# One hybrid decoder layer in fp32 on one core: asking for the weight residues of three projection groups one or two chunks earlier

## The chip, the core and the metric

The kernel runs on one core of one Trainium2 chip. The metric is the device time of one execution in microseconds. A core has a matmul engine (PE), a vector engine (DVE), a scalar engine (ACT), a general engine (POOL) and a queue that issues the loads (SP). Each works through its own list of instructions in order, and they wait for each other through semaphores.

## What is computed

The reference is one decoder layer for 256 tokens of width 1024, in fp32. Two causal token mixers share one RMS-normed input and one combined projection: A, eight heads that share one key and value head and attend to the 64 keys per token that a small indexer picks; B, eight heads with keys and values of their own (with 256 tokens there is one block, so B is plain causal attention). Their outputs are concatenated and go through one output projection; then come a SwiGLU feed-forward block, a gated embedding and a last norm. Cut to what matters here:

```
a = rmsnorm(h, g_attn)
proj = a @ w_in                      # 2500 columns: qa ka va qi ki wi qb kb vb
y_a = dsa_attention(qa, ka, va, qi, ki, wi)   # relu indexer, top 64 keys, softmax
y_b = moba_attention(qb, kb, vb)              # causal softmax
h = h + concat(y_a, y_b) @ w_out
h = h + (silu(f @ w_gate) * (f @ w_up)) @ w_down      # f = rmsnorm(h)
h = h + sigmoid(u @ w_ple_gate) * (p @ w_ple_proj)    # u = rmsnorm(h)
out = rmsnorm(h, g_final)
```

## The kernel before

Every fp32 matrix product is done in three passes of a reduced format: a matrix is split into `hi`, its cast to that format, and `lo`, the residue `raw - hi`; the product is hi x hi + hi x lo + lo x hi. So each weight chunk takes three steps ahead of the matmuls. SP loads `raw` from memory (line 120, at most 1 MB), ACT casts it to `hi` (line 131), DVE subtracts and leaves `lo` (line 158). A chunk of 2048 columns is cast and subtracted in two halves of 1024, which are the rows `128x1024` of the views; the first half serves the first two row blocks k of the chunk, the second half the other two. Chunks have a fixed list (`CHUNKS`), and `raw`, `hi` and `lo` have three buffers each, used in turn.

Chunks 5 and 6 are projection group 2 (kb), 7 and 8 group 3 (vb), 9 and 10 group 4 (qa), 11 is the weight `pp` of the embedding and 12 to 15 are `wo`, the output projection. So `lo8` is the residue of group 3's second chunk, `hi12` the cast of the first `wo` chunk, and so on.

`need(kind, k0)` is called where the matmuls of a chunk are written. It calls `load(i + LOOK)`, which records the loads and casts up to three chunks ahead, and `split(i)`, which records the residues up to chunk i and no further. PE's order is that of the code, since only PE is scheduled by hand; on DVE and ACT a scheduler places instructions by the order in which the code records them and by its own estimate of when each can run. So the place where `split` is called decides where DVE's residue work stands among the other work of DVE.

Around the change the code runs group 1 (qb), evacuates group 0, runs group 2 (kb), turns its result (`evac_rope`, lines 325 to 332, the rope of kb), runs group 3 (vb) and then group 4 (qa). Within a group, PE does six matmuls of 512 columns for each of eight steps (two row blocks, three passes, one half t of the tokens). Between the steps of groups 3 and 4 stand parts of the attention, hung in by a table (`at_tick`): transposes of `qb`, of the indexer's heads (`tidx`) and of `kb`, the indexer's products (`qki`, then `rel` on ACT and `score` on DVE), the logits of B's three units (`qk_b`, then `lg`, `pr` and the transposes `pt_b`). The top-k of the indexer's scores (lines 427 and 428: MAX of eight keys and their replacement, eight rounds for each half of the tokens) makes the mask `dmask` for A's units, which follow while the output projection runs (`qk_a`, `lg_a`, `pr_a`, `pt_a`).

Of the kernel before, what the change touches and what calls it, by code (L numbers as in the profile page):

```python
# [62 lines left out]
def layer_kernel(  # L63
# [39 lines left out]
    def load(upto):  # L103
        while state["hi"] <= min(upto, len(chunks) - 1):
            i = state["hi"]
            kind, k0, src, nk, cw = chunks[i]
            n = nk * cw
            if nk == 1:
                raw = a2.tile([P, n], F32, tag="pr", name=f"raw{i}", bufs=4)
            elif kind == "g1":  # L110

                if k0 < 6:
                    if k0 == 2:
                        state["g1"] = act.tile([P, 2048], F32, tag="yH", name="raw_g1")
                    raw = state["g1"][:, (k0 - 2) // 2 * n : (k0 // 2) * n]
                else:
                    raw = act.tile([P, n], F32, tag="yL", name=f"raw{i}")
            else:
                raw = wp.tile([P, 2048], F32, tag="raw", name=f"raw{i}")
            nc.sync.dma_start(raw[:, :n], src)  # L120
            if i == len(chunks) - 1:
                hi = state["ff"].tile([P, 2048], F32R, tag="hidH", name=f"hi{i}", bufs=1)
            elif nk == 1:
                hi = a2.tile([P, n], F32R, tag="rt2", name=f"hi{i}")
            elif kind == "g1":
                hi = at.tile([P, n], F32R, tag={2: "qbT", 4: "kbT", 6: "vb"}[k0], name=f"hi{i}")
            else:
                hi = wp.tile([P, 2048], F32R, tag="hi", name=f"hi{i}")
            step = cw * max(1, min(nk, 1024 // cw))
            for o in range(0, n, step):  # L130
                nc.scalar.copy(hi[:, o : o + step], raw[:, o : o + step])  # L131
            tiles[i] = (raw, hi)
            state["hi"] += 1

    def split(upto):
        load(upto)
        while state["lo"] <= min(upto, len(chunks) - 1):
            i = state["lo"]
            kind, k0, src, nk, cw = chunks[i]
            n = nk * cw  # L140
            raw, hi = tiles.pop(i)
            if i == len(chunks) - 1:
                lo = state["ff"].tile([P, 2048], F32R, tag="hidL", name=f"lo{i}", bufs=1)
            elif nk == 1:
                lo = a2.tile([P, n], F32R, tag="r0", name=f"lo{i}")
            elif kind == "g1":
                if k0 < 6:
                    if k0 == 2:
                        state["g1l"] = act.tile([P, 2048], F32R, tag="pp", name="lo_g1")
                    lo = state["g1l"][:, (k0 - 2) // 2 * n : (k0 // 2) * n]  # L150
                else:
                    lo = at.tile([P, n], F32R, tag="idxT", name=f"lo{i}")
            else:
                lo = wp.tile([P, 2048], F32R, tag="lo", name=f"lo{i}")
            step = cw * max(1, min(nk, 1024 // cw))
            for o in range(0, n, step):
                e = o + step
                nc.vector.tensor_tensor(  # L158
                    lo[:, o:e], raw[:, o:e], hi[:, o:e].bitcast(F32), op=ALU.subtract
                )  # L160
            ready[i] = (
                hi[:, :n].rearrange("p (k w) -> p k w", k=nk),
                lo[:, :n].rearrange("p (k w) -> p k w", k=nk),
            )
            state["lo"] += 1

    def need(kind, k0):
        i = index[(kind, k0)]
        load(i + LOOK)
        split(i)  # L170
        return ready[i]

    def mm3(ps, aH, aL, wH, wL, start, stop):
# [96 lines left out]
    with actx:  # L270
# [29 lines left out]
        def piece(g, pss, k, ts):  # L300

            if g == 0:
                (wH, wL), r = g0[k], slice(None)
            else:
                c0 = max(c[1] for c in chunks if c[0] == f"g{g}" and c[1] <= k)
                wH, wL = need(f"g{g}", c0)
                wH, wL = wH[:, k - c0, :], wL[:, k - c0, :]
            width = wH.shape[1]
            for n, (aT, wT) in enumerate(((XH, wH), (XL, wH), (XH, wL)) if len(ts) > 1 and k else ((XH, wH), (XH, wL), (XL, wH))):
                for t in ts:  # L310
                    nc.tensor.matmul(  # L311
                        pss[t][:, :width], aT[:, k, tsl(t)], wT,
                        start=k == 0 and n == 0, stop=k == KD - 1 and n == 2,
                    )
# [274 lines left out]
        for t in range(NT):  # L589
            for c in range(2):  # L590
                ps = acc(f"pp{t}{c}")
                wH, wL = need("pp", 0)
                cc = slice(c * NQ, (c + 1) * NQ)
                for k in range(2):
                    mm3(ps, pTH[:, k, tsl(t)], pTL[:, k, tsl(t)], wH[:, k, cc], wL[:, k, cc], k == 0, k == 1)
                nc.scalar.copy(pp[:, t, cc], ps)
                tick("pp", 2 * t + c)
# [4 lines left out]
        def wo_mms(kk, t, c):  # L602
            wH, wL = need("wo", kk - kk % 2)
            cc = slice(c * NQ, (c + 1) * NQ)
            mm3(po[(t, c)], yH[:, kk, tsl(t)], yL[:, kk, tsl(t)], wH[:, kk % 2, cc], wL[:, kk % 2, cc], kk == 4, kk == 3)
# [6 lines left out]
        i = 0  # L612
# [276 lines left out]
```

## Time and profile before

| what | value |
|---|---|
| median of 3 runs | 341.28 us (340.81 to 341.32) |
| the profiled execution | 342.88 us |
| its span, first to last instruction | 341.0 us |
| mean granted clock of PE | 0.984 |
| PE busy | 327.8 us (96%) |
| DVE busy | 227.7 us (67%) |
| ACT busy | 174.3 us (51%) |

The span is what the views show; the execution's own time has 1.88 us more around it. The granted clock is 1 where PE runs at 2.4 GHz and 0.5 where it runs at 1.2. In the timeline a row has the start in us from the span's start, the duration, the engine, the line, the operation, out<-in, the shapes, the number of instructions in the row, and in brackets the idle time ahead of it with what ended it. Matmuls overlap, so the distance of two starts, and not the duration, is what one costs.

### The profile page before, as it was taken

To read this page: it belongs to the slowest core of one execution; us is meant where nothing else is said; L and a number is where in the kernel's file an instruction comes from. 1 tells how busy PE (TensorE), PEld (TensorE's weight loads), DVE (VectorE), ACT (ScalarE), POOL (GpSimd) and SP (SyncE) were. 2 spreads that over 40 slices of the span, in tenths; PEclk is the share of its full clock that TensorE was granted. 3 is DMA by queue.
4 is the path that set the end of the run, shared out by engine and by line. 5 is a ranking of instruction groups with operands and counts; after the bars stand their busy time and mean duration, and the time that the engine had idled before them with its cause. 6 is when DMAs were issued, how large, how long until landed. Compare 5 with 4: busy or idle time off the path is not lost.

```text
span 341.0 us, 4346 instructions
## 1 busy us (share of the span) xinstructions
PE 327.8 (96%) x1637; PEld 266.8 (78%) x1637; DVE 227.7 (67%) x464; ACT 174.3 (51%) x278; POOL 5.6 (2%) x16
## 2 busy tenths in 40 slices
PE   8999969979999999999999999999999999999992
PEld 7888847757777788888888888888878888888891
DVE  3958995999988597465535644655465343469884
ACT  4957335388687286345433553455352424237623
POOL 2001000000000000000000000000000000000110
PEclk9999978999999999999999999999999999999997
DMA  7995918300643316663466436634663646460012
GB/s 252 418 380 189 359 47 350 124 3 0 209 162 123 125 27 284 246 243 106 158 234 235 144 117 244 246 114 145 236 244 127 235 139 235 136 238 4 0 40 85
DMA packets 10389, 59.71 MB, mean 175 GB/s; under 512 B 1280, under 2 KB 1536, under 8 KB 4096
## 3 DMA queue, kind: packets, MB, share of 16 engines
q1 hardware_dynamic: 10224, 59.24, 48.0%
q8 instruction: 13, 0.21, 0.3%
q10 hardware_dynamic: 144, 0.20, 0.2%
q14 instruction: 8, 0.07, 0.1%
HBM read 58.38 MB, written 1.05 MB: 174 GB/s over the span
## 4 chain that ended last, share of the span: by engine, by line
PE 76%; DVE 11%; ACT 2%; issue 1%; ACTq 0%; DVEq 0%
PE ff L174 12%; PE ff L176 12%; PE ff L175 12%; PE wd L174 6%; PE wd L175 6%; PE wd L176 6%; PE g L311 3%; DVE lo L158 3%; PE pg L176 2%; PE pg L174 2%; PE pg L175 2%; PE wo L174 2%; PE wo L176 2%; PE wo L175 2%; PE hidt L677 1%; ACT hi L131 1%
## 5 line engine op out<-in xcount | busy, mean ns | idle before, releaser
L158 DVE TENSOR_TENSOR lo<-raw,hi 128x1024 fp32r<-128x1024 f32 (+1 forms) x99 | 116.3, 1208 | 67.6 <-ACT hi L131 67.5
L131 ACT CAST hi<-raw 128x1024 fp32r<-128x1024 f32 (+1 forms) x99 | 98.5, 1041 | 92.1 <-PE ff L176 42.4
L174 PE MATMUL ff<-hi,FH 128*128 128x512 f32 x176 | 69.6, 396 | 0.0
L176 PE MATMUL ff<-hi,FL 128*128 128x512 f32 x176 | 68.6, 390 | 0.0
L175 PE MATMUL ff<-lo,FH 128*128 128x512 f32 x176 | 68.5, 389 | 0.0
L176 PEld LDWEIGHTS ff<-hi,FL 128*128 128x128 f32 x176 | 33.0, 188 | 7.1
L175 PEld LDWEIGHTS ff<-lo,FH 128*128 128x128 f32 x176 | 33.1, 188 | 6.4
L174 PEld LDWEIGHTS ff<-hi,FH 128*128 128x128 f32 x176 | 33.1, 188 | 6.4
L174 PE MATMUL wd<-hi,hidH 128*128 128x512 f32 x88 | 35.2, 400 | 0.0
L175 PE MATMUL wd<-lo,hidH 128*128 128x512 f32 x88 | 34.9, 397 | 0.0
L176 PE MATMUL wd<-hi,hidL 128*128 128x512 f32 x88 | 34.6, 393 | 0.0
L311 PE MATMUL g<-hi,XH 128*128 128x512 f32 x64 | 26.5, 420 | 0.0
L311 PE MATMUL g<-lo,XH 128*128 128x512 f32 x56 | 22.7, 411 | 3.4 <-DVE lo L158 3.4
L311 PE MATMUL g<-hi,XL 128*128 128x512 f32 x64 | 25.8, 408 | 0.0
L174 PEld LDWEIGHTS wd<-hi,hidH 128*128 128x128 f32 x88 | 16.5, 188 | 4.2 <-issue 0.3
L176 PEld LDWEIGHTS wd<-hi,hidL 128*128 128x128 f32 x88 | 16.5, 188 | 4.1
L175 PEld LDWEIGHTS wd<-lo,hidH 128*128 128x128 f32 x88 | 16.5, 188 | 3.6
L706 ACT ACTIVATE sg<-ff,f_y 128x512 f32<-128x512 f32 (+1 forms) x12 | 7.8, 648 | 17.3 <-PE ff L176 17.3
L711 DVE SCALAR_TENSOR_TENSOR hid<-ff,f_y,sg 128x512 f32<-128x512 f32 (+1 forms) x12 | 8.4, 703 | 12.1 <-PE ff L176 10.0
L311 PEld LDWEIGHTS g<-lo,XH 128*128 128x128 f32 x56 | 11.1, 198 | 5.7 <-DVE lo L158 3.7
L681 DVE TENSOR_TENSOR hidL<-hidt,hidH 128x512 fp32r<-128x512 f32 (+1 forms) x12 | 7.7, 642 | 11.4 <-ACT hidH L680 11.3
L311 PEld LDWEIGHTS g<-hi,XH 128*128 128x128 f32 x64 | 12.5, 195 | 3.1 <-issue 0.7
(201 smaller groups left out, 457.5 us busy)
## 6 DMA issues: line engine op xcount, KB each, us to landing
raw<-in_w_dram SPq DMA_DIRECT2D x48, 1024.0 KB, 4.9
a<-in_xa_dram SPq DMA_DIRECT2D x8, 354.5 KB, 6.6
raw_g<-in_w_dram SPq DMA_DIRECT2D x2, 512.0 KB, 7.7
h<-in_x_dram SPq DMA_DIRECT2D x1, 1024.0 KB, 11.9
raw<-in_w_dram SPq DMA_DIRECT2D x2, 256.0 KB, 4.3
raw<-in_w_dram SPq DMA_DIRECT2D x1, 512.0 KB, 8.3
gBffn<-in_g_ffn_dram SPq DMA_DIRECT2D x1, 512.0 KB, 5.9
gBple<-in_g_ple_dram SPq DMA_DIRECT2D x1, 512.0 KB, 5.7
```

The lines of the kernel that those rows point to most:

```text
L131: nc.scalar.copy(hi[:, o : o + step], raw[:, o : o + step])
L158: nc.vector.tensor_tensor(lo[:, o:e], raw[:, o:e], hi[:, o:e].bitcast(F32), op=ALU.subtract)
L174: nc.tensor.matmul(ps, aH, wH, start=start, stop=False)
L175: nc.tensor.matmul(ps, aH, wL, start=False, stop=False)
L176: nc.tensor.matmul(ps, aL, wH, start=False, stop=stop)
L311: nc.tensor.matmul(pss[t][:, :width], aT[:, k, tsl(t)], wT, start=k == 0 and n == 0, stop=k == KD - 1 and n == 2,)
L677: nc.tensor.transpose(pt[:, i * P : (i + 1) * P], hid[:, i * P : (i + 1) * P], ident)
L681: nc.vector.tensor_tensor(hidL[:, kk, tsl(t)], pv, hidH[:, kk, tsl(t)].bitcast(F32), op=ALU.subtract)
L706: nc.scalar.activation(sg[:, :w], ps[:, :w], AF.Silu, scale=rf[t])
L711: nc.vector.scalar_tensor_tensor(hid[:, :w], up, rf[t], pgu[("s", t)][:, :w], op0=ALU.mult, op1=ALU.mult)
```

## The change

The request for residues in `need` goes further for the groups 2, 3 and 4: one chunk ahead when the group's first chunk is asked for, two chunks ahead when its second is.

```diff
     def need(kind, k0):
         i = index[(kind, k0)]
         load(i + LOOK)
-        split(i)
+        ahead = (1 if k0 == 0 else 2) if kind in ("g2", "g3", "g4") else 0
+        split(i + ahead)
         return ready[i]
```

The residues of chunks 5 to 7 are asked for by other lines already, so the first call with an effect is the one of group 2's second chunk, which records `lo8` ahead of the rope of kb. Group 3's second chunk records `lo9` and `lo10`, group 4's second `lo11` and `lo12`. No instruction is added or taken away; the lists of SP, POOL and PE keep their order. Lines behind line 169 are numbered one higher after the change.

On DVE, at the end of group 2, before (`r01` and `r0b` are the rope of group 0's result, `kb0` and `kb1` that of group 2's for the two halves of the tokens):

```order
L329 TENSOR_TENSOR r01_t2_436<-g0_1_259,kcs_246 128x6x32
L325 TENSOR_TENSOR kb0_502<-g2_0_442,kcs_246 128x512
L332 TENSOR_TENSOR r0b_253<-r0b_253,r01_t2_436 128x384
L326 TENSOR_TENSOR kb0_t2_503<-g2_0_442,kcs_246 128x8x32
L373 COPY r0b_253<-r0b_253 128x64
L329 TENSOR_TENSOR kb0_t2_503<-g2_0_442,kcs_246 128x8x32
L325 TENSOR_TENSOR kb1_508<-g2_1_443,kcs_246 128x512
L332 TENSOR_TENSOR kb0_502<-kb0_502,kb0_t2_503 128x512
L326 TENSOR_TENSOR kb1_t2_509<-g2_1_443,kcs_246 128x8x32
L329 TENSOR_TENSOR kb1_t2_509<-g2_1_443,kcs_246 128x8x32
L158 TENSOR_TENSOR lo8_562<-raw8_444,hi8_446 128x1024
L332 TENSOR_TENSOR kb1_508<-kb1_508,kb1_t2_509 128x512
```

And after the change, at the same place:

```order
L330 TENSOR_TENSOR r01_t2_436<-g0_1_259,kcs_246 128x6x32
L158 TENSOR_TENSOR lo8_478<-raw8_444,hi8_446 128x1024
L333 TENSOR_TENSOR r0b_253<-r0b_253,r01_t2_436 128x384
L158 TENSOR_TENSOR lo8_478<-raw8_444,hi8_446 128x1024
L374 COPY r0b_253<-r0b_253 128x64
L326 TENSOR_TENSOR kb0_505<-g2_0_442,kcs_246 128x512
L327 TENSOR_TENSOR kb0_t2_506<-g2_0_442,kcs_246 128x8x32
L330 TENSOR_TENSOR kb0_t2_506<-g2_0_442,kcs_246 128x8x32
L326 TENSOR_TENSOR kb1_511<-g2_1_443,kcs_246 128x512
L333 TENSOR_TENSOR kb0_505<-kb0_505,kb0_t2_506 128x512
```

Both halves of `lo8` moved from behind the rope of kb to ahead of it.

On DVE, ahead of the first tile of B's probabilities that PE transposes, before (`score0` and `score1` are the indexer's scores of the two halves of the tokens, `lg_b` the masked logits, `pr_b000` the probabilities):

```order
L428 MATCH_REPLACE score0_601<-m8_0_825,score0_601 128x128
L427 MAX m8_1_885<-score1_635 128x8
L427 MAX m8_0_825<-score0_601 128x8
L428 MATCH_REPLACE score1_635<-m8_1_885,score1_635 128x256
L428 MATCH_REPLACE score0_601<-m8_0_825,score0_601 128x128
L427 MAX m8_1_885<-score1_635 128x8
L427 MAX m8_0_825<-score0_601 128x8
L428 MATCH_REPLACE score1_635<-m8_1_885,score1_635 128x256
L474 RECIPROCAL rc_b00_686<-su_b00_685 128x4
L464 ISA lg_b100_727,mn_b10_724<-qk_b100_718,cadd_236 128x256
L464 ISA mn_b10_724 128x1
L476 TENSOR_TENSOR pr_b000_688<-pr_b000_688,rc_b00_686 128x512
```

After the change:

```order
L465 ISA lg_b001_702,mn_b00_687<-qk_b001_678,cadd_236 128x128
L465 ISA mn_b00_687 128x1
L158 TENSOR_TENSOR lo12_755<-raw12_627,hi12_629 128x1024 x2
L475 RECIPROCAL rc_b00_689<-su_b00_688 128x4
L465 ISA lg_b100_730,mn_b10_727<-qk_b100_721,cadd_236 128x256
L465 ISA mn_b10_727 128x1
L477 TENSOR_TENSOR pr_b000_691<-pr_b000_691,rc_b00_689 128x512
```

The top-k rounds that stood here stand behind B's probabilities now, and `lo12` stands in their place. Counted over the whole way up to `pr_b000`, six MAX and five MATCH_REPLACE of score0 and four of each of score1 moved behind it.

On ACT, around the end of group 3, before:

```order
L572 ACTIVATE vb_255<-g3_0_514,rx_y_334 128x512
L131 CAST hi11_559<-raw11_557 128x1024 x2
L412 ACTIVATE rel0_0_605<-qki0_0_602 128x256
L412 ACTIVATE rel0_1_610<-qki0_1_607 128x256
L572 ACTIVATE vb_255<-g3_1_515,rx_y_334 128x512
```

After the change:

```order
L573 ACTIVATE vb_255<-g3_0_517,rx_y_334 128x512
L573 ACTIVATE vb_255<-g3_1_518,rx_y_334 128x512
L131 CAST hi11_562<-raw11_560 128x1024 x2
L413 ACTIVATE rel0_0_611<-qki0_0_608 128x256
L413 ACTIVATE rel0_1_616<-qki0_1_613 128x256
```

The second half of `vb` moved ahead of the cast `hi11`.

## Rows read from the trace of the kernel before

**Rows 1.** Busy time of each engine, its share, its instructions.

```profile
PE 327.8 (96%) x1637; PEld 266.8 (78%) x1637; DVE 227.7 (67%) x464; ACT 174.3 (51%) x278; POOL 5.6 (2%) x16
```

**Rows 2.** What PE waited for: us in total, times, longest.

```profile
PE g L311 <- DVE lo L158: 3.4, 1, 3.4
PE pt_b L483 <- DVE pr_b L476: 1.8, 1, 1.8
```

**Rows 3.** Timeline of PE in groups 3 and 4.

```profile
41.79 0.48 PE L311 MATMUL g<-hi,XH 128*128 128x512 f32 x1
42.11 0.40 PE L311 MATMUL g<-lo,XH 128*128 128x512 f32 x1
...
43.62 0.48 PE L311 MATMUL g<-hi,XH 128*128 128x512 f32 x1
47.51 0.79 PE L311 MATMUL g<-lo,XH 128*128 128x512 f32 x1 [3.41 <-DVE lo L158]
...
53.71 0.48 PE L311 MATMUL g<-hi,XH 128*128 128x512 f32 x1
...
57.30 0.50 PE L311 MATMUL g<-hi,XH 128*128 128x512 f32 x1
```

**Rows 4.** Stretches: busy of PE, PEld, DVE, ACT, POOL; granted clock, DMA share, GB/s.

```profile
46.60:46.70 0.10, 0.00 (x0) 0.00 (x0) 0.10 (x1) 0.00 (x0) 0.00 (x0) 0.79 0.00 0
...
47.50:50.00 2.50, 2.49 (x6) 1.90 (x7) 2.50 (x3) 0.00 (x0) 0.00 (x0) 0.50 0.03 7
...
53.40:53.50 0.10, 0.10 (x3) 0.10 (x2) 0.10 (x1) 0.00 (x0) 0.00 (x0) 0.58 0.00 0
...
70.50:72.30 1.80, 0.03 (x1) 0.02 (x1) 1.80 (x9) 1.80 (x11) 0.00 (x0) 1.00 0.02 5
```

**Rows 5.** Timeline of DVE from the rope of kb to `lo11`.

```profile
42.55 0.68 DVE L325 TENSOR_TENSOR kb<-g,kcs 128x512 f32<-128x512 f32 x1
...
46.24 1.21 DVE L158 TENSOR_TENSOR lo<-raw,hi 128x1024 fp32r<-128x1024 f32 x1
...
47.98 5.75 DVE L158 TENSOR_TENSOR lo<-raw,hi 128x1024 fp32r<-128x1024 f32 x5
...
57.83 2.36 DVE L158 TENSOR_TENSOR lo<-raw,hi 128x1024 fp32r<-128x1024 f32 x2 [3.50 <-ACT hi L131]
```

**Rows 6.** Timeline of PE: transposes of the probabilities of B and A.

```profile
72.31 0.63 PE L483 MATMUL pt_b<-ident,pr_b 128*128 128x128 f32 x4 [1.78 <-DVE pr_b L476]
...
98.95 0.60 PE L483 MATMUL pt_a<-ident,pr_a 128*128 128x128 f32 x4
```

**Rows 7.** Timeline of DVE: top-k rounds, logits, probabilities.

```profile
66.12 0.61 DVE L427 MAX8 m<-score 128x8 f32<-128x256 f32 x2
66.65 0.07 DVE L428 MATCH_VALUE_LOAD score<-m,score 128x8 f32 x1
...
67.03 0.28 DVE L464 CUSTOM_DVE_ANT_0 lg_b<-qk_b,cadd 128x128 f32<-128x128 f32 x1
...
68.72 0.09 DVE L428 MATCH_VALUE_LOAD score<-m,score 128x8 f32 x1
...
68.98 0.61 DVE L427 MAX8 m<-score 128x8 f32<-128x256 f32 x2
...
71.47 0.69 DVE L476 TENSOR_TENSOR pr_b<-pr_b,rc_b 128x512 f32<-128x512 f32 x1
...
97.33 0.69 DVE L476 TENSOR_TENSOR pr_a<-pr_a,rc_a 128x512 f32<-128x512 f32 x1
```

**Rows 8.** Timeline of ACT: the cast `hi11`.

```profile
56.75 2.00 ACT L131 CAST hi<-raw 128x1024 fp32r<-128x1024 f32 x2 [0.68 <-PE g L311]
```

**Rows 9.** Loads of 1 MB chunks: times, KB each, median us to landing.

```profile
raw<-in_w_dram SPq DMA_DIRECT2D x48, 1024.0 KB, 4.9
```

**Rows 10.** Longer stretches, columns as in rows 4.

```profile
60.00:70.00 10.00, 10.00 (x63) 7.70 (x62) 9.71 (x52) 4.70 (x12) 0.00 (x0) 1.00 0.31 106
...
120.00:341.00 221.00, 214.36 (x995) 176.61 (x993) 128.35 (x183) 101.37 (x124) 2.58 (x2) 0.99 0.46 164
```

## The prediction

> **What bounds the kernel now.** I read the busy shares first: the matmul engine PE works for 96% of the span and the vector engine DVE for 67% [rows 1]. So at most a few per cent are PE's idle time, and the view that lists what PE waited for says where it lies: one wait of 3.4 us of the projection matmuls for a `lo` piece of DVE, and one of 1.8 us of a transpose for `pr_b` [rows 2]. The change is about the first. The timeline of PE shows it: group 3's first `hi` matmul of its second chunk starts at 43.62, the `lo` matmul behind it only at 47.51 [rows 3]. The table by stretches shows what the wait brings with it. PE's granted clock stands at 1.00 (2.4 GHz) while it waits, falls in the slice 46.60 to 46.70 after PE has done nothing since 44.10, is 0.50 (1.2 GHz) when the matmuls resume, and comes back in the slice 53.40 to 53.50, while they run [rows 4]. The timeline of DVE shows why `lo8` was late: DVE was not idle, it worked through the ropes of `kb` from 42.55 on, started `lo8` at 46.24, and then did the next five pieces in one go; later, at 57.83, it had stood idle for 3.50 us [rows 5]. So the wait is one of order on DVE, not of amount.
>
> **What the wait costs.** At full clock one unit of PE (six matmuls and a set of transposes) takes 43.62 - 41.79 = 1.83 us, and a group's second matmul starts 42.11 - 41.79 = 0.32 behind its first [rows 3]. Without a wait the `lo` matmul would start at 43.62 + 0.32 = 43.94 instead of 47.51: 3.57 us. From 47.51 to 53.71 PE does the rest of that unit and one whole unit more. At full clock that is (43.62 - 42.11) + 1.83 = 3.34 us, and it took 6.20: 2.86 us for the clock. Together PE could be 6.43 us ahead at 53.71.
>
> **Does the residue come in time?** In the new order the first half of `lo8` stands where `kb0` stood. It starts at 42.55 and takes the 1.21 us of the row at 46.24, so it ends at 43.76; PE went on 0.06 after the end of that piece (47.45 to 47.51), so it is served at 43.82 and needs it at 43.94. That is a spare of 0.12 us; if it is missed, PE waits by the miss alone. The second half follows after one short addition, before 45.5, and is wanted two units after 43.62, at 47.28. The input of the piece, `hi8`, is not late: the scalar engine casts in order, and in the trace of before DVE went from `kb` straight to `lo8`. The ropes of `kb` slip behind the two pieces, and `lo9` follows them. Group 4 needs its first half, which in before was the second of the five pieces from 47.98 on (5.75 us, so 1.14 each) and ended at 47.98 + 1.14 + 1.21 = 50.33; nothing more stands ahead of it now, so it is no later. PE gets to group 4 at 57.30 - 6.43 = 50.87 [rows 3, 5]. No new wait there, with 0.5 us to spare.
>
> **What moves to the path instead.** The requests two chunks ahead also pull `lo11` (for `pp`) and `lo12` (for `wo`) forward in DVE's order, and push top-k rounds back. The next place where PE waits for DVE is the first transpose of `pr_b`: it comes to it at 72.31 - 1.78 = 70.53 and goes on at 72.31 [rows 6]. If PE is 6.43 ahead it comes at 64.10. For DVE I count its work from 42.55 to the end of `pr_b000`, 71.47 + 0.69 = 72.16, in before: 29.61 us, of which 3.50 are the idle time at 57.83; 26.11 stay [rows 5, 7]. In the new order six MAX and five MATCH_REPLACE of score0 and four of each of score1 no longer stand ahead of it. A pair of MAX takes 66.65 - 66.12 = 0.53, a MATCH_REPLACE of 256 keys 67.03 - 66.65 = 0.38, one of 128 keys 68.98 - 68.72 = 0.26 [rows 7]: 4 x 0.53 + 2 x 0.20 + 4 x 0.38 + 5 x 0.26 = 5.34 us go. The two halves of `lo12` come, 2.28 us. So `pr_b000` ends at 42.55 + 26.11 - 5.34 + 2.28 = 65.60, and with the 0.15 from 72.16 to 72.31 PE goes on at 65.75: it waits 1.65 instead of 1.78, and is 72.31 - 65.75 = 6.56 ahead behind it.
>
> Two new waits sit in DVE's queue. `lo12` needs `hi12`, which the scalar engine casts behind the first two exponentials; behind `lo12` stand the reciprocals and products that make `pr_b`, and PE waits for these. It costs from nothing (the cast is done) up to one half cast, 1 us [rows 8]. `lo11` needs `hi11`, which like in before starts when group 3's last matmul has read the buffer [rows 8], now also behind `vb1`, one pass over 512 columns. Its data is asked for when `lo8` is done, at about 45.4 instead of 47.98 + 1.21 = 49.19, and lands 4.9 us later by the median of such loads [rows 9], at 50.3, when group 3 ends at about 56.75 - 6.43 = 50.32. No price, or as much as the landing is late. The other side of the bounds: the 26.11 hold short pauses of DVE (60 to 70 us: busy 9.71 of 10 [rows 10]) that the pulled pieces can fill, up to 0.5 us. So PE's lead behind `pr_b` is 5.5 to 7.1; I stay near 6.56.
>
> The top-k rounds come due in the stage of unit A. Its transpose of `pr_a001` ran at 98.95 in before without a wait, and DVE ended that tile at 97.33 + 0.69 = 98.02 [rows 6, 7]. From `pr_b000` on DVE had 25.86 us of work until there. Now 5.34 us of top-k are added, the two halves of `lo12` and two of `lo14` (which now stand behind) are gone, 4.56 us, and two more score tiles of 256 keys stand ahead, each at most twice the 0.28 of a 128-key one, say 0.7 together. That gives 65.60 + 25.86 + 5.34 - 4.56 + 0.7 = 92.94, served at 93.1, where PE comes at 98.95 - 6.56 = 92.39. A new wait of 0.7 us, or of 0.3 if half a microsecond of short pauses goes. I take 0.35, the lead is then 6.2 us. Behind 120 us nothing moves: PE's order is the same and it is busy for 214.4 of 221 us [rows 10], so the lead is kept to the end.
>
> **The sum.** 3.57 + 2.86 + 0.13 (the wait at `pr_b`, 1.78 to 1.65) - 0.35 = 6.2 us. The profiled execution took 342.88 us (341.0 of span and 1.88 around it) and would take 336.7. The median of the three runs, 341.28, lies 1.60 below it; I carry that over: 335.1 us.
>
> **Rivals.**
> (a) DVE becomes the bound. In the stretch behind the change DVE is nearly always busy (9.71 of 10 us from 60 on [rows 10]). If each later wait of PE simply grows until DVE is through the same work, all that is won is DVE's own idle time, 3.50 us: 337.8. Against it: the order shows work leaving DVE's stretch ahead of `pr_b`, and PE took the tiles of unit A without waiting. The Trainium skill (Perfetto Trace Analysis, "Identifying the Most-Contended Engine" and "Optimization Strategy") has the engine with the highest occupancy as the one that decides, and says that this can change from one regime to the next; by that rule this stretch would belong to DVE and this rival would be the result. The trace agrees only in part, since PE is busy for 10.00 of the same 10 us. Chance 0.12.
> (b) The clock falls once more. If the wait at `pr_b` grows from 1.65 to the 3.4 us of the one at `lo8`, in which the clock fell, PE does its next matmuls at 0.50 again and as much is lost, 2.86 us, beside some of the wait itself: 341.28 - 6.2 + 2.86 = 337.9 with the clock alone. Against it: through the wait of 1.78 us the clock stayed at 1.00 [rows 4]. The Trainium skill (TensorE: Matmul & The Clock Gate, "A second HAM failure mode: psum-queue depth-cycling") says that frequent short idles between groups of matmuls can make the clock swing; by it the short waits left here would be enough and this rival would hold. No stretch of this trace shows that. Chance 0.06.
> (c) The postponed top-k rounds land on the path, and the kernel is slower. The mask of unit A is ready only when the rounds are done. If nothing hides the 5.34 us, PE stands still that long, the clock falls with it (2.86), and 8.20 against 6.43 makes 341.28 + 1.8 = 343.1. It decides from a new wait of 3.6 us at unit A on, since 3.57 + 2.86 makes up for the whole gain. Against it: `lo12` and `lo14`, 4.56 us, leave the same stretch. Chance 0.04.
> (d) Nothing happens, because PE's first matmul waits for something that is as late as before, such as the cast or a buffer of `lo`. Against it: the order shows `lo8` ahead of all the ropes of `kb`. 341.3, chance 0.03.
> (e) The wait at `pr_b` goes too, and all of 6.43 + 1.78 is won: 333.1. It needs 1.65 us less DVE work than counted. Chance 0.03.
>
> **How the numbers follow.** The forecast has 0.72, with 334.3 to 336.1 as its own range (leads of 7.0 and 5.2). About 0.2% is what a measurement here can tell, 0.7 us. Faster: 0.72 + 0.12 + 0.06 + 0.03 = 0.93; same 0.03; slower 0.04. The range runs from 334.1, a little above (e), to 338.0, which takes in (a) and (b).
>
> **What would show it.** PE's list of waits no longer names `lo` with more than 0.3 us; both sets of transposes of `tidx` are done by 47.3 (43.62 and two units) at clock 1.00, and no stretch between 40 and 100 us has 0.50. `pr_b` is transposed near 65.8 after a wait of 1 to 2 us, and a wait of under 1 us for `pr_a` appears near 93. Idle time of DVE before `lo11` is gone. I am wrong if a `lo` or `hi` piece holds up PE in group 3 or 4, if the wait at `pr_b` reaches that of `lo8` in before, or if PE waits for a mask of unit A.

## The result and the profile after

The changed kernel takes 336.16 us (median of 4 runs, 335.19 to 336.31), the kernel before on the same chip 341.29 us (340.81 to 341.32): a ratio of 0.9847, 95% interval 0.9827 to 0.9867, or 5.1 us less. A second set of runs gave 335.78 against 341.09 (0.9833, 0.9809 to 0.9856), 5.3 us. Forecast were 335.1 and 6.2 us: the right mechanism, with the size some 1 us too large. The first set's interval, 4.5 to 5.9 us less, leaves 6.2 out, the second's, 4.9 to 6.5, does not; 336.16 lies just above the forecast's own range (334.3 to 336.1) and 335.78 in it. The profiled execution took 335.19 us with a span of 333.4.

The busy shares, answering to [rows 1], and what PE waited for, answering to [rows 2] (us in total, times, longest):

```profile
PE 324.3 (97%) x1637; PEld 264.4 (79%) x1637; DVE 227.0 (68%) x464; ACT 175.2 (53%) x278; POOL 5.6 (2%) x16
```

```profile
PE pt_b L484 <- DVE rc_b L475: 0.8, 1, 0.8
...
PE pt_a L484 <- DVE pr_a L477: 0.7, 2, 0.4
```

No `lo` piece is in the list any more. Of the two waits for `pr_a` one, 0.37 us at the last tile of unit A, stands in the list of before as well (0.4, once); the other is new. The timeline of PE at the places of [rows 3, 6]:

```profile
42.51 0.60 PE L380 MATMUL tr<-ident,qb 128*128 128x128 f32 x4
42.86 0.48 PE L312 MATMUL g<-hi,XH 128*128 128x512 f32 x1
43.18 0.40 PE L312 MATMUL g<-lo,XH 128*128 128x512 f32 x1
...
46.16 0.60 PE L380 MATMUL tidx<-ident,r0b 128*128 128x128 f32 x4
46.52 0.48 PE L312 MATMUL g<-hi,XH 128*128 128x512 f32 x1
...
49.47 0.72 PE L409 MATMUL qki<-idxT 64*128 64x128 f32 x8
...
64.17 0.63 PE L484 MATMUL pt_b<-ident,pr_b 128*128 128x128 f32 x4 [0.83 <-DVE rc_b L475]
...
89.00 0.60 PE L484 MATMUL pt_a<-ident,pr_a 128*128 128x128 f32 x4
91.31 0.63 PE L484 MATMUL pt_a<-ident,pr_a 128*128 128x128 f32 x4 [0.31 <-DVE pr_a L477]
```

The `lo` matmul stands 0.32 behind its `hi` matmul, as in any other unit, where before it stood 3.89 behind. The stretches, answering to [rows 4] (PE, PEld, DVE, ACT, POOL, granted clock, DMA share, GB/s), have PE busy for all of the 20 us at 1.00, and the clock stays there through the wait at `pr_b` too:

```profile
40.00:60.00 20.00, 20.00 (x120) 15.52 (x120) 19.69 (x47) 11.53 (x21) 0.00 (x0) 1.00 0.65 242
...
63.10:64.10 1.00, 0.24 (x2) 0.00 (x0) 1.00 (x5) 1.00 (x6) 0.00 (x0) 1.00 0.63 66
```

DVE, answering to [rows 5, 7], does both halves of `lo8` ahead of the rope of kb; its idle time of 3.50 us ahead of `lo11` is gone, and what is left is short:

```profile
41.06 1.21 DVE L158 TENSOR_TENSOR lo<-raw,hi 128x1024 fp32r<-128x1024 f32 x1
...
42.66 1.21 DVE L158 TENSOR_TENSOR lo<-raw,hi 128x1024 fp32r<-128x1024 f32 x1
...
43.90 0.68 DVE L326 TENSOR_TENSOR kb<-g,kcs 128x512 f32<-128x512 f32 x1
...
52.46 0.35 DVE L418 SCALAR_TENSOR_TENSOR score<-rel,w,init 128x128 f32<-128x128 f32 x1 [0.23 <-ACT rel L413]
...
60.65 2.36 DVE L158 TENSOR_TENSOR lo<-raw,hi 128x1024 fp32r<-128x1024 f32 x2 [0.23 <-ACT hi L131]
...
63.34 0.69 DVE L477 TENSOR_TENSOR pr_b<-pr_b,rc_b 128x512 f32<-128x512 f32 x1
```

PE's lead between the two traces on record: at the start of group 3's unit it is already 43.62 - 42.86 = 0.76, which is the start of that execution and not the change. Two units later it is 53.71 - 46.52 = 7.19, so the change gave 6.43 there, which is 3.57 + 2.86 to the hundredth. At `pr_b` another 0.95 comes (the wait is 0.83 instead of 1.78), at `pr_a001` 0.50 go (98.95 - 91.31 = 7.64, against 72.31 - 64.17 = 8.14). Less the start that is 6.9 us between these two executions. The medians are only 5.1 apart, so one of the two was not a usual one. Which, and in what, is the first question for the experiments.

### The profile page after: what moved, and what is told of

It reads as the page before. It is cut to its first block, busy times and chain, and to the rows that moved or that the text cites. A ratio compares the mean times of both kernels' runs of the same rounds, so it can differ in the third digit from the quotient of the medians.

```text
span 333.4 us, 4350 instructions
## 1 busy us (share of the span) xinstructions
PE 324.3 (97%) x1637; PEld 264.4 (79%) x1637; DVE 227.0 (68%) x464; ACT 175.2 (53%) x278; POOL 5.6 (2%) x16
## 4 chain that ended last, share of the span: by engine, by line
PE 81%; DVE 12%; ACT 4%; issue 1%; ACTq 0%
PE g L312 13%; PE ff L175 12%; PE ff L177 12%; PE ff L176 12%; PE wd L175 6%; PE wd L176 6%; PE wd L177 6%; DVE lo L158 3%; PE pg L177 2%; PE pg L175 2%; PE pg L176 2%; ACT hi L131 2%; PE hidt L678 1%; DVE score L429 1%; DVE m L428 1%
## 5 line engine op out<-in xcount | busy, mean ns | idle before, releaser
L312 PE MATMUL g<-hi,XH 128*128 128x512 f32 x64 | 25.8, 408 | 0.0
L312 PE MATMUL g<-hi,XL 128*128 128x512 f32 x64 | 24.8, 393 | 0.0
L312 PE MATMUL g<-lo,XH 128*128 128x512 f32 x56 | 21.6, 391 | 0.0
L312 PEld LDWEIGHTS g<-hi,XL 128*128 128x128 f32 x64 | 12.0, 188 | 2.7
```

The costliest lines, as they stand in the source:

```text
L312: nc.tensor.matmul(pss[t][:, :width], aT[:, k, tsl(t)], wT, start=k == 0 and n == 0, stop=k == KD - 1 and n == 2,)
```

## The experiments

**How executions of the kernel before differ.** No edit. Three more executions of it were profiled; they are called again 1, again 2 and again 3 here.

> The kernel before once more, to see how far its executions differ and where. Its profiled execution took 342.88 us, its runs 341.3. Theory S (the start differs): from the first matmul to group 3 (41.79 us in the trace on record) an execution can be 1 to 2 us shorter, the wait for lo8 stays at 3.4 us and the half-clock stretch at 2.86 us of loss; mean clock 0.984. Theory K (the clock differs): the half-clock stretch is shorter in the usual execution, by up to 1.6 us, and the mean clock is higher, near 0.99. Time 341.3 in both.

> The kernel before, one more profile, to see where its clock falls. On record are one execution in which it fell in the wait for lo8 (342.88 us, 2.86 us lost behind it) and one in which it stayed at 1.00 through that wait (2.97 us) and fell in the later one for pr_b (340.69 us, about 1.5 us lost). Theory P: it falls in one of the two waits each time, the wait for pr_b among them, and never in both. Rival: it falls in none or in both. Time 339.3 to 342.8.

> The same once more, with the same two theories: half clock behind the wait for lo8 (and a time near 342) or behind the one for pr_b (near 340.7).

The three profiled executions took 340.69, 340.20 and 341.18 us (the median of the runs taken with again 1 is 341.12 us, 339.35 to 342.72). In the trace on record, PE does the last transposes of `qb` ahead of the wait and the first `qki` behind it at:

```profile
43.27 0.60 PE L379 MATMUL tr<-ident,qb 128*128 128x128 f32 x4
...
56.64 0.72 PE L408 MATMUL qki<-idxT 64*128 64x128 f32 x8
```

PE in again 1:

```profile
42.46 0.60 PE L380 MATMUL tr<-ident,qb 128*128 128x128 f32 x4
...
46.27 0.50 PE L312 MATMUL g<-lo,XH 128*128 128x512 f32 x1 [2.97 <-DVE lo L158]
...
47.54 0.60 PE L380 MATMUL tidx<-ident,r0b 128*128 128x128 f32 x4
...
52.66 0.72 PE L409 MATMUL qki<-idxT 64*128 64x128 f32 x8
...
68.60 0.90 PE L484 MATMUL pt_b<-ident,pr_b 128*128 128x128 f32 x4 [2.07 <-DVE pr_b L477]
...
71.86 0.78 PE L484 MATMUL pt_b<-ident,pr_b 128*128 128x128 f32 x4
```

Its stretches:

```profile
43.30:46.20 2.90, 0.00 (x0) 0.00 (x0) 2.90 (x6) 1.84 (x3) 0.00 (x0) 1.00 0.00 0
...
69.00:71.50 2.50, 2.50 (x9) 2.01 (x8) 2.30 (x10) 2.18 (x9) 0.00 (x0) 0.50 0.02 7
```

Here the clock stays at 1.00 through the whole wait for `lo8`, and `tidx` follows 1.27 us behind the `lo` matmul instead of the 2.30 of the trace on record. It falls right behind the later wait, the one at `pr_b` (1.00 until 68.8, while PE resumes at 68.60), and two sets of transposes stand 3.26 apart there instead of 1.85. In again 2 it falls while PE waits for `lo8`, as in the trace on record, but is back sooner:

```profile
42.58 0.60 PE L380 MATMUL tr<-ident,qb 128*128 128x128 f32 x4
...
46.36 0.80 PE L312 MATMUL g<-lo,XH 128*128 128x512 f32 x1 [2.94 <-DVE lo L158]
...
54.06 0.72 PE L409 MATMUL qki<-idxT 64*128 64x128 f32 x8
```

```profile
45.00:46.00 1.00, 0.00 (x0) 0.00 (x0) 1.00 (x2) 0.26 (x1) 0.00 (x0) 0.93 0.00 0
...
49.00:50.00 1.00, 1.00 (x7) 0.91 (x6) 1.00 (x2) 0.40 (x1) 0.00 (x0) 0.86 1.06 164
```

In again 3:

```profile
43.30 0.60 PE L380 MATMUL tr<-ident,qb 128*128 128x128 f32 x4
...
47.08 0.50 PE L312 MATMUL g<-lo,XH 128*128 128x512 f32 x1 [2.94 <-DVE lo L158]
...
55.05 0.72 PE L409 MATMUL qki<-idxT 64*128 64x128 f32 x8
```

```profile
44.00:47.00 3.00, 0.14 (x1) 0.00 (x0) 3.00 (x7) 1.98 (x3) 0.00 (x0) 1.00 0.00 0
47.00:48.00 1.00, 0.92 (x3) 0.78 (x4) 1.00 (x3) 0.00 (x0) 0.00 (x0) 0.75 0.00 0
48.00:50.00 2.00, 2.00 (x8) 1.61 (x8) 2.00 (x3) 0.00 (x0) 0.00 (x0) 0.50 0.49 70
...
50.00:51.00 1.00, 1.00 (x4) 0.81 (x4) 1.00 (x2) 0.59 (x1) 0.00 (x0) 0.55 0.40 139
```

it falls only when the matmuls have resumed, at about 47.5. One ledger for all (the first line is the start of the last transposes of qb, the others are distances on PE, read from the same rows in each trace):

| us | before, on record | again 1 | again 2 | again 3 | after, on record | after again |
|---|---|---|---|---|---|---|
| last transposes of qb | 43.27 | 42.46 | 42.58 | 43.30 | 42.51 | 42.81 |
| from there to the first `qki` | 13.37 | 10.20 | 11.48 | 11.75 | 6.96 | 6.96 |
| wait at `pr_b` | 1.78 | 2.07 | 1.78 | 1.79 | 0.83 | 0.84 |
| first to third `pt_b` | 7.56 | 9.14 | 7.55 | 7.55 | 7.55 | 7.56 |
| `pt_a000` to `pt_a001` | 1.83 | 1.84 | 1.83 | 1.83 | 2.31 | 2.34 |
| span | 341.0 | 338.9 | 338.4 | 339.4 | 333.4 | 333.7 |

The lines add up: again 2 against after again is 4.52 + 0.94 - 0.51 - 0.23 (start) = 4.72, and the spans are 4.7 apart; again 3 gives 4.79 + 0.95 - 0.51 + 0.49 = 5.72 against 5.7. The late residue alone costs 10.20 - 6.96 = 3.24, where the clock stayed. The clock costs 1.28 and 1.55 in again 2 and 3 (11.48 and 11.75 less 10.20), 1.58 at the other place in again 1 (9.14 - 7.56), and 2.86 in the execution on record. What differs is how long the matmuls ran at 0.50: from 47.51 to about 53.5 on record, 6.0 us, but only to about 49.3 in again 2 (2.9 us) and from about 47.5 to 50.9 in again 3 (3.4 us). Each time a little under half of that is lost. So the profile on record was the dearest of the four: a wait 0.4 us longer, and a clock that came back later.

Theory P (one of the two waits each time) held in these four executions, but not its times: near 342 us was expected with the fall behind `lo8`, and 340.20 and 341.18 came. S was right that the start can differ (up to 0.8 us) and wrong that the wait stays at 3.4 (2.9 to 3.0); K was right about the shorter half-clock stretch.

The executions without a trace have a mean granted clock on record too, and it tells how common each kind is. Of the 55 others of the kernel before that have one, ten have 0.983 or 0.984, as the execution on record, and take 341.55 to 342.76 us; forty have 0.988 to 0.993 and take 340.2 to 341.73; five have 0.996 and take 339.16 to 340.04. The mean also holds the end of the kernel, where PE is done, so it sorts only roughly; but executions as dear as the one on record are about one in five. The five at 0.996 may have lost the clock in neither wait, which P does not allow; none of them was traced, so that is not shown.

**The changed kernel again.** No edit.

> The changed kernel once more. Its profiled execution took 335.19 us, three others 336.2. Time 336.2 (335.2 to 336.5), ratio to before 0.985. Theory S: an execution of 336.2 us starts its group 3 about 1 us later than 41.03 and is the same behind it. Rival W: the start is the same and the wait for the first pr_b is longer, 1.8 us instead of 0.83.

335.78 us (335.51 to 335.9), ratio 0.9833 (0.9809 to 0.9856). W falls: the wait at `pr_b` is 0.84 again. S is not settled: the profiled execution took 335.51 us, not the 336.2 that S speaks of, and its start is 0.30 us later (the table). Nothing between 40 and 120 us has less than 1.00.

**Only `lo8` early.**

```diff
-        ahead = (1 if k0 == 0 else 2) if kind in ("g2", "g3", "g4") else 0
+        ahead = 2 if (kind, k0) == ("g2", 4) else 0
```

> Only the residue of group 3's second chunk is asked for early (group 2's second chunk asks two ahead); groups 3 and 4 ask for nothing ahead. Theory F (the forecast's: all gain comes from lo8, and the chunks pulled further forward only decide how large the later waits for DVE are): no wait for a lo piece over 0.3 us in group 3, clock 1.00, and a time within 1 us of the changed kernel's 336.2. Rival D (the gain needs lo10 to lo12 pulled forward too, since without them DVE is bound by its order): PE waits for pr_b by 3 us or more, the lead shrinks to DVE's idle time of 3.5 us, and the time is 337.8 or more.

335.70 us (335.49 to 336.21), ratio 0.9834 (0.981 to 0.9857): the same as the whole change. F held, D falls: no `lo` piece is in PE's list of waits, and the clock is 1.00 from 40 to 120 us. The waits for the probabilities in its trace:

```profile
PE pt_a L484 <- DVE pr_a L477: 1.0, 2, 0.8
...
PE pt_b L484 <- ACT pr_b L471: 0.5, 1, 0.5
```

The order of DVE moves here by itself: with `lo8` early the scheduler puts six MAX and six MATCH_REPLACE of the top-k behind `pr_b000` (ten and nine in the changed kernel), and `lo12` stays behind.

**Only groups 3 and 4 ahead.**

```diff
-        ahead = (1 if k0 == 0 else 2) if kind in ("g2", "g3", "g4") else 0
+        ahead = (1 if k0 == 0 else 2) if kind in ("g3", "g4") else 0
```

> The other part of the change alone: groups 3 and 4 ask ahead, group 2 does not, so lo8 stays behind the rope of kb and lo10 to lo12 come early. Theory F: the wait for lo8 is 3.0 to 3.4 us as in before, nothing is won there, and the time is 341.1 within 0.7. Rival D (the pulled pieces have a worth of their own, since they fill DVE's idle time): faster by 1 us or more, 340.0 or less, through a shorter wait for pr_b. Rival C (lo12 ahead of pr_b delays it): slower by up to its 2.3 us, 343.4, through a longer one.

343.36 us (340.2 to 344.1) against 341.08, ratio 1.0054 (1.0028 to 1.008): slower by 2.3 us by the medians, by 1.0 to 2.7 by the ratio. C named the cause. DVE, then PE, then the stretch behind it:

```profile
68.09 2.36 DVE L158 TENSOR_TENSOR lo<-raw,hi 128x1024 fp32r<-128x1024 f32 x2 [0.19 <-ACT hi L131]
70.37 0.17 DVE L475 RECIPROCAL rc_b<-su_b 128x4 f32<-128x4 f32 x1
```

```profile
71.61 1.08 PE L484 MATMUL pt_b<-ident,pr_b 128*128 128x128 f32 x4 [2.60 <-DVE rc_b L475]
...
75.02 0.60 PE L484 MATMUL pt_b<-ident,pr_b 128*128 128x128 f32 x4
```

```profile
72.00:74.50 2.50, 2.50 (x9) 2.11 (x8) 2.19 (x9) 2.08 (x7) 0.00 (x0) 0.50 0.87 357
```

`lo12` stands right ahead of the reciprocal that makes `pr_b`, the wait is 2.60, and the clock falls in it although it had fallen behind `lo8` already: 3.41 between the two sets instead of 1.85. 2.60 - 1.88 (the mean of the waits in again 1 to 3) and 1.56 are 2.3. That C's 2.3 came out is luck: it stood for the work of the two `lo12` pieces and was to be all wait, while the wait grew by 0.7 and the rest is clock. It does not come each time: seven of the ten executions have a mean clock of 0.980 to 0.986 and take 342.95 to 344.1 us, the other three 0.990 to 0.995 and 340.2 to 341.58, as in the kernel before.

**The wait kept, the clock held up.** The kernel before, with matmuls on zeros in the wait:

```diff
+FILL = 14
...
+        def fill():
+            fps = aux("fill")
+            for j in range(FILL):
+                nc.tensor.matmul(fps, fz[:, :P], fz, start=j == 0, stop=j == FILL - 1)
...
+                    if g == 3 and k == 4 and n == 1 and t == 0:
+                        fill()
                     nc.tensor.matmul(
```

> The kernel before, with 14 matmuls of 128x512 on zeros between group 3's hi and lo matmul of the second chunk: PE works through most of the 3.4 us in which it waits for lo8 there (14 x 0.23 = 3.2 us), and the residues stay as late as before. It separates the clock from the wait. Theory F: the granted clock stays at 1.00, the 6.2 us behind the wait take 3.34, and the time is 341.3 - 2.86 = 338.4. Rival K (in the usual execution the clock costs less than in the profiled one): 339.5 to 340.5. Rival N (the clock falls anyway, or DVE takes the lead back at pr_b): 341.3, with the wait for pr_b 2.9 us longer in the second case.

338.87 us (338.77 to 339.23), ratio 0.9927 (0.9907 to 0.9946). PE (13 of the 14 are in the records):

```profile
42.99 0.60 PE L389 MATMUL tr<-ident,qb 128*128 128x128 f32 x4
...
43.67 3.19 PE L306 MATMUL fill<-fz 128*128 128x512 bf16 x13
46.77 0.50 PE L321 MATMUL g<-lo,XH 128*128 128x512 f32 x1
...
53.17 0.72 PE L418 MATMUL qki<-idxT 64*128 64x128 f32 x8
...
70.06 0.63 PE L493 MATMUL pt_b<-ident,pr_b 128*128 128x128 f32 x4 [1.17 <-ACT pr_b L480]
```

The `lo` matmul is as late as ever (53.17 - 42.99 = 10.18, the 10.20 of again 1, whose clock stayed there), the clock is 1.00 from 43 to 120 us, and 2.2 us are won by medians. Not all of that is clock. DVE's order moved too (five MAX and five MATCH_REPLACE behind `pr_b000`): PE takes the first tile of `pr_b` without a wait and waits for the second, 1.3 us by the starts (the first two `pt_b` stand 3.17 apart, 1.85 without a wait) instead of 1.9, so about 1.6 are the clock's. That is rival K's 0.8 to 1.8, with 0.6 from `pr_b` on top, and not F's 2.9 (its clock of 1.00 came, its time did not); it agrees with the 1.28 to 1.58 of again 1 to 3. What is left to the changed kernel, 338.87 - 335.78 = 3.1 us, is the price of the late residue at full clock.

**What is left behind the change.** Two moves of transposes on PE, then one alone, then that one with `lo8` alone:

```diff
-        at_tick(("g4", 5), tp(B[0], 0))
+        at_tick(("g4", 6), tp(B[0], 0))
-        at_tick(("wb", 4), tp(A[0], 1))
-        at_tick(("wb", 5), A[0].pv, A[2].qk)
+        at_tick(("wb", 5), tp(A[0], 1))
+        at_tick(("wb", 5), A[2].qk, A[0].pv)
```

> The changed kernel with two sets of transposes hung in one unit of matmuls later (B's first pr_b beside its second; A's second pr_a after the unit, with A's last logits ahead of the product with va), so that PE has matmuls of its own where it waited 0.84 for pr_b and 0.35 for pr_a. Theory F (these waits are what is left of DVE's lateness, and PE is the bound): both waits go, 335.8 - 1.0 = 334.8. Rival (a) (DVE is the bound behind the change): the waits come back at the next tiles and the time stays at 335.8.

> The changed kernel with only B's first set of pr_b transposes hung one unit of matmuls later; unit A stands as it was. The run with both moves took 335.31 us and had a new wait of 1.08 us for pT_a. Theory F: the wait for pr_b is 0.4 us, the one at pr_a001 0.35 to 0.8, no wait for pT_a, and the time 335.8 - 0.45 = 335.3, the same as with both moves. Rival (a) (what is won at pr_b comes back whole at pr_a001): 335.8.

> The kernel that asks ahead for lo8 alone (335.7 us), with B's first transposes one unit later as well. Theory F: its wait of 0.53 us for pr_b goes or moves to the second tile, and the time is 335.2 to 335.7. Rival (a): its wait at pr_a001, 0.77 us, grows by as much and the time stays at 335.7.

335.31 us (ratio 0.9824, 0.9809 to 0.984), 335.14 (0.9838, 0.9819 to 0.9858) and 335.68 (0.9846, 0.9825 to 0.9867): by the ratios none can be told from the changed kernel's 0.9833, so F and (a) are not settled by the time. The 334.8 that F gave for both moves did not come: the wait for `pr_b` moved to the second tile (0.38 us), and a wait of 1.08 us for `pT_a` appeared, which the expectation had not. In the trace of the one with B's move alone:

```profile
65.26 1.27 PE L484 MATMUL pt_b<-ident,pr_b 128*128 128x128 f32 x8
...
91.77 0.63 PE L484 MATMUL pt_a<-ident,pr_a 128*128 128x128 f32 x4 [0.75 <-DVE pr_a L477]
```

the wait at `pr_b` is gone (F had left 0.4 of it) and the one at `pr_a001` has grown from 0.35 to 0.75. By the starts, PE is 0.71 us earlier at the third `pt_b` than in after again, counted from the last transposes of `qb`, and 0.26 earlier at `pr_a001`: more than half of what was won comes back. With `lo8` alone the wait at `pr_b` goes too and the one at `pr_a001` is 0.85 instead of 0.77, less than (a) says, but the time stays. By median the three lie 0.1 to 0.6 us below the 335.78 of the changed kernel, which comes from another set of runs.

## Why the prediction was right, and where its size was off

**The wait was one of order.** Right. `lo8` went ahead of kb's rope and the wait was gone; the run with `lo8` alone has the whole gain.

**The price of the wait, 3.57 + 2.86.** Between the two executions that were profiled it is exact (6.43). As the price in a usual execution it was too high: 3.2 for the residue (3.24 and 3.22) and about 1.5 for the clock (1.28, 1.55, 1.58). This is the step that failed in its size: the sum was made against an execution of 342.88 us, 1.60 above its median, and "I carry that over" took for granted that the 1.60 would stay in the changed kernel. They lay in the very stretch that the change takes out (2.86 - 1.5 of clock, 3.57 - 3.24 of wait: 1.7). Again 3, with the same start (43.30 against 43.27), shows it directly: its span is 1.6 us shorter, and so is its way from the last transposes of `qb` to the first `qki` (11.75 against 13.37).

**Does the residue come in time?** Right, with more room than the 0.12 us forecast: in the trace after, the first half ends at 42.27 and is wanted at 43.18. DVE reached that place 42.86 - 41.06 = 1.80 ahead of PE's unit, against 1.07 in the trace of before; in again 1 to 3 that lead is 1.52 to 1.55. No new wait in groups 3 and 4.

**The wait at `pr_b`, 1.65 forecast, 0.83 found.** DVE's work from `lo8` to the end of `pr_b000` was counted as 65.60 - 42.55 = 23.05 and is 63.34 + 0.69 - 41.06 = 22.97, short pauses included. The totals agree, but in part by luck: the 22.97 hold a pause of 0.23 us ahead of `score`, where DVE waits for ACT's `rel`, so the work itself was 0.3 shorter than counted. That is 0.3 of the 0.82 us by which the wait came out shorter. DVE's start gives the other 0.5: it was 0.73 earlier against PE, but the pause takes up 0.23 of that. Earlier still would not have helped: in after again DVE leads by 2.2 us, and the pause is longer by as much as the lead, while the wait at `pr_b` stays at 0.84:

```profile
52.76 0.35 DVE L418 SCALAR_TENSOR_TENSOR score<-rel,w,init 128x128 f32<-128x128 f32 x1 [0.63 <-ACT rel L413]
```

**The pulled pieces.** The prediction put the postponed top-k down to the requests two chunks ahead. Only in part: the scheduler postpones six of the ten rounds of MAX for `lo8` alone. `lo12` ahead of `pr_b` cost nothing here (335.78 us with it, 335.70 without), and 0.7 us of wait and a second half-clock stretch where the wait for `lo8` was left in.

**The new wait at `pr_a001`, 0.35 forecast, 0.48 and 0.51 found.** Right in place, a little small in size (these are by the starts; the rows name 0.31 and 0.35 as idle time), and the counted 0.7 was the upper end.

**The rivals.** (a), DVE as the bound, is no account of the change: 5.1 to 5.3 us are more than DVE's idle time of 3.50, which itself is only 1.03, 2.06 and 2.33 us in again 1 to 3. That PE took the tiles of unit A without waiting, as was held against (a), is not quite so: the 0.37 us at the last of them was there before. DVE shows as the bound in the last microsecond, where a wait taken away at `pr_b` comes back in part at `pr_a001`. That is how far the rule on the engine with the highest occupancy (the Trainium skill, Perfetto Trace Analysis, "Identifying the Most-Contended Engine") goes here. The same section judges TensorE's headroom by MFU and the busy share of its weight loads (7.70 of the 10 us in [rows 10]), not by that of its matmuls (10.00), which the prediction set against DVE's 9.71; so by weight loads the rule does name DVE there, and the gain came by order all the same. (b) did not come: the clock stays at 1.00 through the waits of 0.3 to 0.8 us. Its mechanism is real, though, as the run without the early `lo8` shows: 2.60 us at `pr_b` and the clock fell again. (c), (d) and (e) did not come.

Put with the usual prices the sum is 3.23 + 1.47 + (1.88 - 0.84) - 0.51 = 5.2 us; measured were 5.1 and 5.3. These prices are read from the same runs, so this shows where the time went and is no test of its own. Against it the forecast's 6.2 is only 1.0 off because errors cancel, which is luck: the price of the wait was 1.7 too high, the gain at `pr_b` 0.9 too low, the loss at `pr_a001` 0.2 too low.

## What to carry to other kernels

Before a stall is priced, compare the profiled execution's time and mean granted clock with those of the other executions: if it is slower, ask which part of the surplus lies in the stall itself, because that part is not won twice. Price the wait at full clock and the clock behind it as two terms, and take the second as a range from nothing to its full length unless several executions show it. Of a request that is moved earlier for many pieces, one piece may carry all the gain, and the others can cost where they land ahead of something urgent.

## What the runs showed of the hardware

The same wait of 2.9 to 3.0 us had three outcomes in executions of one kernel: no fall of the granted clock (again 1), a fall about 0.4 us after the matmuls had resumed (again 3), and a fall ahead of that (again 2: 0.93 in the stretch 45 to 46, the matmuls resume at 46.36). A wait of 2.07 us had a fall behind it in one execution, and waits of 1.78 and 1.79 had none in three. So the length of the wait alone did not decide. What a fall cost was a little under half of the time that matmuls ran at 0.50 (2.86 of 6.0 us, 1.28 of 2.9, 1.55 of 3.4). Matmuls on zeros in the wait went with a clock of 1.00 in the one kernel that had them.
